# Block two's expert layer: fp32 up-projections for the small experts, one weight matrix per transfer, four fixed experts

## The chip, the cores and the metric

The kernel runs on one core of one Trainium2 chip. The metric is the device time of one execution in microseconds (us). Before the change it is 2680.42 us, the median of three runs (2679.35 to 2682.9). A core has TensorE (PE for its matmuls, PEld for its loads of the stationary operand), VectorE (DVE), ScalarE (ACT), GpSimd (POOL) and SyncE (SP, which here only issues transfers).

## The reference, cut to what matters

Two transformer blocks run one after the other on 1024 tokens of width 1024, all in float32. Each ends in a layer of experts. The change touches the one of block two: 32 experts in 4 groups of 8, two experts for every token, hidden width 256.

```python
def hier_moe_2(x, wg, bg, we, be, w_gate, w_up, w_down):
    g_logits = xf @ wg + bg                      # a group for each token
    grp = jnp.argmax(g_logits, axis=-1)
    e_in = ...                                   # the logits of its 8 experts
    top_v, top_i = lax.top_k(e_in, 2)
    combine = p_grp * jax.nn.softmax(top_v)
    ...
    hb = jax.nn.silu(xb @ w_gate[e]) * (xb @ w_up[e])   # 1024 -> 256, twice
    return hb @ w_down[e]                                # 256 -> 1024
    # each row times its weight, then added to its token
```

The weights of one expert are three matrices of 1 MB each, so 32 experts read 100 MB.

## The kernel before

`run` goes through both blocks in program order; each engine executes its own list in that order. The expert layer (`moe`, line 1799 on) works through the experts in a fixed order `Lay.order`. Every place p in it has a fixed capacity of rows, `caps[p]`. The first `NP` places are the experts 0, 1, 2 themselves ("fixed"), so their weights can be asked for before the routing is known. The other places hold the remaining experts sorted by their number of rows; which expert that is stands in `idx`, and SP must first read it (`values_load`, line 1784) to form the address. Rows beyond a capacity are left to a loop behind (`moe_rest`).

In block two the capacities are 128, 128, 128 (fixed), 192, three of 128, four of 96, six of 80 and fifteen of 64. The order of work is 0, 1, 2, then alternately a larger and a small one (3, 17, 4, 18, ..., 16, 30) and at last 31. A place of 192 is worked as two units of 128 and 64 rows, so there are 18 larger units and 15 small experts (capacity 64, `whole`).

What an expert costs on each engine:

- `gather` (line 1805): POOL fetches the token rows.
- `xT` (line 1815): 8 PE transposes into PSUM; ACT and DVE take them out as a high part and the remainder, both in fp32r, a 4-byte float type whose matmul is one record in the trace. For a small expert both parts lie side by side, so that one stationary operand of 128 columns holds 64 high and 64 low rows.
- `up` (line 1839): four weight stages. A stage has two chunks of `w_gate` in the first 512 columns and two of `w_up` in the others, by two transfers of 256 KB (2 KB per partition each). `w_split` splits it: ACT writes the high part (line 190), DVE the remainder (line 194). A larger unit takes three matmuls for each of 8 chunks (high by high, high by low, low by high), each 512 columns wide. A small expert takes two for each chunk (both parts at once by high, then by low), 16 of 512 columns.
- `hT` (line 1872): the hidden rows of the expert before are transposed, in the middle of `up`.
- `down` (line 1893): two stages of `w_down` of 512 KB. A larger unit takes 12 matmuls of 512 columns. A small expert uses the unsplit weights in fp32: 4 matmuls of 64 by 512, which TensorE carries out as 8 records. ACT scales both halves of the result (line 1916); POOL adds the rows to the output in memory (`put`, line 1796).

Weight stages are taken from a queue (`w`, line 205). Before each take, `w_ahead` asks for the transfers of up to 20 further stages and has 3 further stages split. All large tiles come from one pool of 42; a tile is handed out again when its last reader is done. During the first experts a generator (`gen`) also puts the rest of the routing between the steps.

Of the kernel before, what the change touches and what calls it, by code (L numbers as in the profile page):

```python
# [14 lines left out]
OP = mybir.AluOpType  # L15
# [61 lines left out]
class Lay:  # L77
# [13 lines left out]

    def whole(self, p):
        return self.add and self.caps[p] <= self.small


    def two(self, p, n):
        return n <= self.small and (not self.add or self.whole(p))

    def units(self, p):
        c, b = self.caps[p], self.base[p]  # L100
# [24 lines left out]
class Kern:  # L125
# [1644 lines left out]
    def plan_moe(self, w1, w3, w2, lay, box):  # L1770
        a1 = w1.rearrange("e (p kk k) h -> e kk p (k h)", kk=4, k=2)
        a3 = w3.rearrange("e (p kk k) h -> e kk p (k h)", kk=4, k=2)
        a2 = w2.rearrange("e (k p) d -> e k p d", k=2)
        lo, hi, al = (lambda t: t[:, 0:512]), (lambda t: t[:, 512:1024]), (lambda t: t[:, 0:1024])
        val = {}

        def src(a, p, k):
            if p < lay.NP:
                return a[p, k]

            def go(dst):
                if p not in val:
                    val.clear()
                    val[p] = self.nc.values_load(
                        box["r"]["idx"][0:1, 2, p:p + 1], engines=[mybir.EngineType.SP], min_val=0, max_val=lay.E - 1)
                self.sy.dma_start(dst, a[bass.ds(val[p], 1), k].rearrange("o p f -> (o p) f"))
            return go
        for p in lay.order:
            for kk in range(4):
                self.w_add([(lo, src(a1, p, kk)), (hi, src(a3, p, kk))], 1024)  # L1790
            for k2 in range(2):
                self.w_add([(al, src(a2, p, k2))], 1024, None if lay.whole(p) else lay.small > 0 and not lay.add and k2 == 1)


    def put(self, ys, ix, y):
# [3 lines left out]
    def moe(self, r, vs, late=None):  # L1799
        ac, ve, te, gp = self.ac, self.ve, self.te, self.gp  # L1800
        lay = r["lay"]
        ys = self.ys[lay.E]
        X, Hn, HT, XG, WK = {}, {}, {}, {}, {}
# [11 lines left out]
        def xT(b):  # L1815
            X[b] = []
            for x, idn, s, n in XG.pop(b):
                if lay.two(b, n):
                    xx = self.t(F32R)[:, :16 * n].rearrange("p (k j n) -> p k j n", k=8, j=2)
                    ps = self.p()  # L1820
                    for k in range(8):
                        te.transpose(ps[:, k * n:(k + 1) * n], x[:, k * 128:(k + 1) * 128], idn)
                    pv = ps[:, :8 * n].rearrange("p (k n) -> p k n", k=8)
                    ac.activation(xx[:, :, 0, :], pv, AF.Copy)
                    ve.tensor_sub(xx[:, :, 1, :], pv, xx[:, :, 0, :])
                    X[b].append((xx, None, s, n))
                    continue
                xh, xl = self.t(F32R), self.t(F32R)
                m = 512 // n
                for q in range(0, 8, m):  # L1830
                    ps, w = self.p(), min(m, 8 - q) * n
                    for k in range(q, min(q + m, 8)):
                        te.transpose(ps[:, (k - q) * n:(k - q + 1) * n], x[:, k * 128:(k + 1) * 128], idn)
                    sl = slice(q * n, q * n + w)
                    ac.activation(xh[:, sl], ps[:, :w], AF.Copy)
                    ve.tensor_sub(xl[:, sl], ps[:, :w], xh[:, sl])
                X[b].append((xh, xl, s, n))

        def up(b, mid=None):
            U = X.pop(b)  # L1840
            P = [self.p() for _ in U]
            for kk in range(4):
                if kk == 2 and mid is not None:
                    hT(mid)
                wh, wl = self.w()
                next(gen, None)
                for k in range(2):
                    for ps, (xh, xl, s, n) in zip(P, U):
                        c = 2 * kk + k
                        if xl is None:  # L1850
                            ops = [(xh[:, c].rearrange("p j n -> p (j n)"), w) for w in (wh, wl)]
                        else:
                            ops = [(x[:, c * n:(c + 1) * n], w) for x, w in ((xh, wh), (xh, wl), (xl, wh))]
                        m = 2 * n if xl is None else n
                        for j, (x, w) in enumerate(ops):
                            rhs = w[:, :1024].rearrange("p (w k h) -> p w k h", w=2, k=2)[:, :, k, :]
                            te.matmul(ps[:m].rearrange("p (w h) -> p w h", w=2), x, rhs,  # L1857
                                      start=c == 0 and j == 0, stop=c == 7 and j == len(ops) - 1)
            Hn[b] = []
            for ps, (_, xl, s, n) in zip(P, U):  # L1860
                h = self.h()
                if xl is None:
                    ac.activation(h[:n], ps[n:2 * n], AF.Copy)
                    ve.tensor_add(h[:n], ps[:n], h[:n])
                    ac.activation(h[:n, 0:256], h[:n, 0:256], AF.Silu)
                    ve.tensor_mul(h[:n, 256:512], h[:n, 0:256], h[:n, 256:512])
                else:
                    ac.activation(h[:n, 0:256], ps[:n, 0:256], AF.Silu)
                    ve.tensor_mul(h[:n, 256:512], h[:n, 0:256], ps[:n, 256:512])
                Hn[b].append((h, s, n))  # L1870

        def hT(b):
            HT[b] = []
            for h, s, n in Hn.pop(b):
                ps = self.p()
                for k in range(2):
                    te.transpose(ps[:, k * n:(k + 1) * n], h[:n, 256 + k * 128:256 + (k + 1) * 128], self.idn[:n, :n])
                if lay.whole(b):
                    t = self.h()[:, :2 * n]
                    ac.activation(t, ps[:, 0:2 * n], AF.Copy)  # L1880
                    HT[b].append((t.rearrange("p (k n) -> p k n", k=2), s, n))
                    continue
                t = self.h(F32R)
                tv = t.rearrange("p (k j n) -> p k j n", k=2, j=2)[:, :, :, :n]
                if lay.two(b, n):
                    tv = t[:, :4 * n].rearrange("p (k j n) -> p k j n", k=2, j=2)
                pv = ps[:, 0:2 * n].rearrange("p (k n) -> p k n", k=2)
                ac.activation(tv[:, :, 0, :], pv, AF.Copy)
                ve.tensor_sub(tv[:, :, 1, :], pv, tv[:, :, 0, :])
                t = tv  # L1890
                HT[b].append((t, s, n))

        def down(b):
            W = WK.pop(b)
            for t, s, n in HT.pop(b):
                p0, p1 = self.p(), self.p()
                for k in range(2):
                    wh, wl = W[k]
                    if lay.whole(b):
                        m, ops = n, [(t[:, k, :], wh)]  # L1900
                    elif lay.two(b, n):
                        m, ops = 2 * n, [(t[:, k].rearrange("p j n -> p (j n)"), w) for w in (wh, wl)]
                    else:
                        hh, hl = t[:, k, 0, :], t[:, k, 1, :]
                        m, ops = n, ((hh, wh), (hh, wl), (hl, wh))
                    for j, (a, w) in enumerate(ops):
                        f, e = k == 0 and j == 0, k == 1 and j == len(ops) - 1
                        self.mm(p0[:m], a, w[:, 0:512], f, e)
                        self.mm(p1[:m], a, w[:, 512:1024], f, e)
                y = self.t()  # L1910
                for ps, o in ((p0, 0), (p1, 512)):
                    if lay.two(b, n) and not lay.add:
                        ac.activation(y[:n, o:o + 512], ps[n:2 * n], AF.Copy)
                        ve.tensor_add(y[:n, o:o + 512], ps[:n], y[:n, o:o + 512])
                    elif lay.add:
                        ac.activation(y[:n, o:o + 512], ps[:n], AF.Copy, scale=r["wc"][:n, s[1], b:b + 1])  # L1916
                    else:
                        ac.activation(y[:n, o:o + 512], ps[:n], AF.Copy)
# [6 lines left out]
        gen = r.pop("gen")  # L1925
# [880 lines left out]
    def run(self):  # L2806
        A = self.A
        l1, l2 = self.lays = (
            Lay(2, [192] * 9 + [128] * 7, [0, 1, 9, 2, 10, 3, 4, 11, 5, 12, 6, 13, 7, 14, 8, 15], 64, False),
            Lay(3, [128] * 3 + [192] + [128] * 3 + [96] * 4 + [80] * 6 + [64] * 15,   # L2810
                [0, 1, 2] + [p + q for p in range(3, 17) for q in (0, 14)] + [31], 64, True))
        b1, b2 = {}, {}
        self.plan_one()
        self.plan_moe(A["exp_w1"][0], A["exp_w3"][0], A["exp_w2"][0], l1, b1)
# [61 lines left out]
```

## Time and profile before

| | before |
|---|---|
| median of 3 runs | 2680.42 us (2679.35 to 2682.9) |
| the profiled execution's own time | 2676.59 us |
| its span, first to last instruction | 2674.5 us |
| PE busy | 2484.8 us (93%) |
| DVE, ACT, POOL busy | 1596.0, 1224.4, 608.1 us |
| granted TensorE clock, mean | 0.970 of full speed |
| bytes moved | 378.38 MB, 141 GB/s over the span |

Block two's experts are the last stage: the first transposes of their rows start at 2305.7 us of the span and the last matmul ends at 2658.0 us. A timeline row gives the start, the length to the end of the last of its instructions, and the idle time ahead of it with what ended it. Matmuls overlap, so the cost of one of a row is the distance from this row's start to the next row's start, divided by the count.

### The profile page before, as it was taken

How to read it: one execution, taken by the hardware profiler on the slowest of the kernel's cores; microseconds unless marked ns; L12 is line 12 of the kernel's file. 1: busy time of each engine (PE TensorE's matmuls, PEld its weight loads, DVE VectorE, ACT ScalarE, POOL GpSimd, SP SyncE). 2: the span in 40 equal slices, each digit the busy share in tenths (PEclk: the TensorE clock that was granted, in tenths of full speed). 3: DMA queues.
4: the chain of work that ended last, by engine and by line, in shares of the span. 5: the costliest groups of instructions: out<-in, count | busy, mean ns of one | idle time of the engine just before them, and what ended most of it. 6: DMA issues, size and time to landing. Idle time of an engine off the chain costs nothing. (4 is left out here: it accounts for less than half of the span.)

```text
span 2674.5 us, 35232 instructions
## 1 busy us (share of the span) xinstructions
PE 2484.8 (93%) x12192; PEld 1912.6 (72%) x12192; DVE 1596.0 (60%) x2659; ACT 1224.4 (46%) x2153; POOL 608.1 (23%) x661
## 2 busy tenths in 40 slices
PE   7999999999999799959999999998999989689996
PEld 7976696778877577758788888996655567555543
DVE  4235338842245688765754563567776645777775
ACT  4336521131123477755344243435555532457775
POOL 1011111000001234441000002153655622223221
PEclk9999999999999899979999999998999989899998
DMA  4000243223251689852221221333222265789996
GB/s 136 25 9 10 56 144 104 83 83 103 95 181 72 197 291 311 299 195 86 63 87 48 71 79 26 94 123 113 96 96 77 76 211 178 244 249 341 344 347 218
DMA packets 245877, 378.38 MB, mean 141 GB/s; under 512 B 31344, under 2 KB 142224, under 8 KB 245696
## 3 DMA queue, kind: packets, MB, share of 16 engines
q1 hardware_dynamic: 216720, 282.42, 32.6%
q0 software_dynamic: 28976, 93.67, 11.0%
q8 instruction: 98, 1.61, 0.2%
q14 instruction: 83, 0.68, 0.1%
HBM read 296.65 MB, written 81.99 MB: 142 GB/s over the span
## 5 line engine op out<-in xcount | busy, mean ns | idle before, releaser
L216 PE MATMUL ps<-s,s 128*128 128x512 f32 (+15 forms) x8744 | 1922.4, 379 | 37.1 <-ACT s L212 7.2
L216 PEld LDWEIGHTS ps<-s,s 128*128 128x128 f32 (+6 forms) x8744 | 1502.6, 187 | 416.5 <-issue 95.1
L194 DVE TENSOR_TENSOR s<-s,s 128x1024 fp32r<-128x1024 f32 (+4 forms) x375 | 461.7, 1252 | 437.5 <-ACT s L190 402.0
L190 ACT ACTIVATE s<-s 128x1024 fp32r<-128x1024 f32 (+3 forms) x393 | 391.2, 1034 | 73.7 <-DMA s<-in_w_up 16.4
L1857 PE MATMUL ps<-s,s 128*128 128x512 f32 (+3 forms) x1200 | 319.0, 413 | 28.5 <-DVE s L194 23.3
L1857 PEld LDWEIGHTS ps<-s,s 128*128 128x128 f32 (+3 forms) x1200 | 213.8, 186 | 101.4 <-DVE s L194 36.7
L370 DVE TENSOR_REDUCE mx<-ps 128x1 f32<-128x512 f32 (+10 forms) x304 | 142.4, 505 | 17.1 <-PE ps L216 15.3
L504 ACT ACTIVATE s<-ps 128x512 f32<-128x512 f32 (+1 forms) x192 | 93.8, 489 | 114.4 <-PE ps L216 110.6
L1153 ACT ACTIVATE s<-ps 128x512 f32<-128x512 f32 x24 | 14.3, 598 | 252.0 <-PE ps L216 252.0
L519 POOL TENSOR_TENSOR s<-s,s 128x512 f32<-128x512 f32 (+1 forms) x64 | 108.3, 1692 | 48.5 <-ACT s L506 25.4
L1796 POOL DMA_INDIRECT out<-s,dst x33 | 54.0, 1635 | 244.6 <-ACT s L1916 144.5
L466 PE MATMUL ps<-s,s 128*64 128x512 f32 (+3 forms) x384 | 84.4, 521 | 0.8 <-DVE mx L370 0.8
L1046 DVE SCALAR_TENSOR_TENSOR s<-s,c,s 128x1024 f32<-128x1024 f32 x60 | 82.7, 1379 | 1.5
L1809 POOL DMA_INDIRECT s<-vs,idx x58 | 73.3, 1263 | 43.9 <-issue 10.4
L212 ACT ACTIVATE s<-s 128x512 fp32r<-128x512 f32 (+2 forms) x49 | 36.8, 775 | 76.7 <-DVE s L2329 35.6
L434 ACT ACTIVATE s<-ps 128x512 f32<-128x512 f32 (+4 forms) x112 | 49.3, 447 | 47.7 <-PE ps L216 46.6
L213 DVE TENSOR_TENSOR s<-s,s 128x512 fp32r<-128x512 f32 (+2 forms) x49 | 41.8, 890 | 45.5 <-ACT s L212 45.5
L303 ACT ACTIVATE s<-s 128x1024 f32<-128x1024 f32 (+1 forms) x25 | 26.4, 1055 | 89.1 <-DVE s L1316 46.4
L2305 ACT ACTIVATE s<-ps 128x512 f32<-128x512 f32 x16 | 9.6, 598 | 100.9 <-PE ps L216 100.9
L2352 POOL DMA_DIRECT2D g1s<-s x8 | 4.3, 539 | 226.1 <-ACT s L2306 216.9
L192 POOL TENSOR_TENSOR s<-s,s 128x1024 fp32r<-128x1024 f32 x18 | 47.1, 2618 | 32.0 <-ACT s L190 31.9
L1181 POOL DMA_DIRECT2D ms<-s x8 | 4.3, 533 | 215.9 <-DVE s L1148 161.4
(501 smaller groups left out, 2417.2 us busy)
## 6 DMA issues: line engine op xcount, KB each, us to landing
s<-in_w_in SPq DMA_DIRECT2D x80, 512.0 KB
s<-in_exp_w SPq DMA_DIRECT2D x128, 256.0 KB
s<-in_w_gate SPq DMA_DIRECT2D x128, 256.0 KB
s<-in_w_up SPq DMA_DIRECT2D x128, 256.0 KB
s<-in_w_down SPq DMA_DIRECT2D x64, 512.0 KB
s<-in_exp_w SPq DMA_DIRECT2D x32, 512.0 KB
s<-in_x SPq DMA_DIRECT2D x16, 512.0 KB
ms<-s POOLq DMA_DIRECT2D x16, 512.0 KB, 5.0
```

The costliest lines, as they stand in the source:

```text
L190: self.ac.activation(hi[:, :n], st[:, :n], AF.Copy)
L194: self.ve.tensor_sub(lo[:, :n], st[:, :n], hi[:, :n])
L216: self.te.matmul(out, lhsT, rhs, start=start, stop=stop)
L370: self.ve.tensor_reduce(mx[:, ii, j:j + 1], ps[:, c0 - s0:c1 - s0], axis=AX.X, op=OP.max)
L434: self.ac.activation(pf[:rows, c:], s[:rows, c:], AF.Exp)
L466: self.te.matmul(o[64 * hh:64 * hh + 64, c:], H["v"](j)[:rows], pf[:rows, hh, c:], start=first, stop=last and not c, skip_group_check=True)
L504: self.ac.activation(pf[:rows, hh, c:], s[:rows, c:], AF.Exp)
L519: eng.tensor_tensor(acc[:rows, :, c:], acc[:rows, :, c:], pf[:rows, :, c:], op=OP.add)
L1046: ve.scalar_tensor_tensor(a[:, :T], gl[:, k:k + T], cw[:, c, k:k + 1], a[:, :T], op0=OP.mult, op1=OP.add)
L1796: self.gp.indirect_dma_start(out=ys, out_offset=bass.IndirectOffsetOnAxis(ap=ix, axis=0), in_=y, in_offset=None, bounds_check=T - 1, oob_i ...
L1809: gp.indirect_dma_start(out=x[:n, :D], out_offset=None, in_=vs, in_offset=bass.IndirectOffsetOnAxis(ap=r["idx"][:n, j, b:b + 1], axis=0))
L1857: te.matmul(ps[:m].rearrange("p (w h) -> p w h", w=2), x, rhs, start=c == 0 and j == 0, stop=c == 7 and j == len(ops) - 1)
```

## The change

In block two only:

1. Small experts compute `up` in fp32 too: their rows are copied once, unsplit (DVE), and their weights of all six stages stay unsplit. A new function `up_add` uses 16 matmuls of 256 columns.
2. A stage is now one matrix: one transfer of 512 KB with four rows (4 KB) per partition, in the order gate, up, gate, up, down, down. `up_add` takes a gate and an up stage together and writes the gate to columns 0 to 255 and the up to 256 to 511 of one PSUM bank. A larger unit so takes 48 matmuls of 256 columns where it took 24 of 512. `hT` stands ahead of the second pair of stages, as before in the middle.
3. The second half of a small expert's result is scaled by DVE, no longer by ACT; the steps that added high and low sums of its `up` fall away.
4. Four experts are fixed, with 128 rows each; the place of 192 is now place 4. The sequence of places is the same, so the 192 comes sixth, behind the first small expert, where it was fourth.

```diff
+            if lay.add:
+                for a, n in ((b1, 0), (b3, 0), (b1, 1), (b3, 1), (a2, 0), (a2, 1)):
+                    self.w_add([(al, src(a, p, n))], 1024, None if lay.whole(p) else False)
+                continue
...
-                if lay.two(b, n):
+                if lay.whole(b):
+                    xx = self.t()[:, :8 * n]
+                    ps = self.p()
+                    for k in range(8):
+                        te.transpose(ps[:, k * n:(k + 1) * n], x[:, k * 128:(k + 1) * 128], idn)
+                    ve.tensor_copy(xx, ps[:, :8 * n])
+                    X[b].append((xx, xx, s, n))
+                    continue
+                if n <= lay.small and not lay.add:
...
+        def up_add(b, U, P, mid):
+            for kk in range(2):
+                if kk and mid is not None:
+                    hT(mid)
+                W = [self.w(), self.w()]
+                for k in range(4):
+                    if k % 2 == 0:
+                        next(gen, None)
+                    c = 4 * kk + k
+                    for ps, (xh, xl, s, n) in zip(P, U):
+                        ops = ((xh, 0),) if lay.whole(b) else ((xh, 0), (xh, 1), (xl, 0))
+                        for j, (x, o) in enumerate(ops):
+                            for h, w in enumerate(W):
+                                self.mm(ps[:n, h * 256:h * 256 + 256], x[:, c * n:(c + 1) * n],
+                                        w[o][:, k * 256:(k + 1) * 256], c + j + h == 0,
+                                        c == 7 and h == 1 and j == len(ops) - 1)
...
+                    elif o and lay.whole(b):
+                        ve.tensor_scalar(y[:n, o:o + 512], ps[:n], r["wc"][:n, s[1], b:b + 1], None, op0=OP.mult)
                     elif lay.add:
                         ac.activation(y[:n, o:o + 512], ps[:n], AF.Copy, scale=r["wc"][:n, s[1], b:b + 1])
...
-            Lay(3, [128] * 3 + [192] + [128] * 3 + [96] * 4 + [80] * 6 + [64] * 15, 
+            Lay(4, [128] * 4 + [192] + [128] * 2 + [96] * 4 + [80] * 6 + [64] * 15,
```

On PE, a small expert's `up` between the transposes of the next larger one (`128x80`) and that one's hidden rows stands thus before; `s_22147` and `s_22148` are the high and low part of a stage, `s_22089` the rows:

```order
L1833 MATMUL ps<-c_74,s_21762 128x80 x8
L1857 MATMUL ps<-s_22147,s_22089 128x512
L1857 MATMUL ps<-s_22148,s_22089 128x512
...
L1857 MATMUL ps<-s_22173,s_22089 128x512
L1857 MATMUL ps<-s_22174,s_22089 128x512
...
L1877 MATMUL ps<-c_74,s_22157 128x80 x2
L1857 MATMUL ps<-s_22180,s_22089 128x512
L1857 MATMUL ps<-s_22181,s_22089 128x512
```

and thus now, with `s_22078` a gate stage and `s_22094` an up stage, both unsplit:

```order
L1842 MATMUL ps<-c_74,s_22022 128x80 x8
L212 MATMUL ps<-s_22078,s_22336 64x256
L212 MATMUL ps<-s_22094,s_22336 64x256
...
L1905 MATMUL ps<-c_74,s_22421 128x80 x2
L212 MATMUL ps<-s_22134,s_22336 64x256
L212 MATMUL ps<-s_22140,s_22336 64x256
```

Each half keeps 8 matmuls; each writes 64 rows by 256 columns where it wrote 128 by 512, and there is no low part.

A larger unit's `up` on PE, its first chunks before (`s_22247` and `s_22248` high and low weights, `s_22198` and `s_22199` high and low rows):

```order
L1857 MATMUL ps<-s_22247,s_22198 80x512
L1857 MATMUL ps<-s_22248,s_22198 80x512
L1857 MATMUL ps<-s_22247,s_22199 80x512
...
L1857 MATMUL ps<-s_22273,s_22198 80x512
L1857 MATMUL ps<-s_22274,s_22198 80x512
```

and its first chunk now (`s_22277` and `s_22278` the gate's parts, `s_22304` and `s_22305` the up's):

```order
L212 MATMUL ps<-s_22277,s_22238 80x256
L212 MATMUL ps<-s_22304,s_22238 80x256
L212 MATMUL ps<-s_22278,s_22238 80x256
L212 MATMUL ps<-s_22305,s_22238 80x256
L212 MATMUL ps<-s_22277,s_22239 80x256
L212 MATMUL ps<-s_22304,s_22239 80x256
```

Every matmul of 512 columns has become two of 256.

On SP, the place where the fixed experts' transfers end, before (`s_19369` is the last `up` stage of expert 2, `s_19559` the first of place 3):

```order
L180 DMA s_19369<-in_w_gate 128x512
L180 DMA s_19369<-in_w_up 128x512
L180 DMA s_19378<-in_w_down 128x1024
L180 DMA s_19380<-in_w_down 128x1024
L1784 TENSOR_LOAD idx
L1784 ISA x2
L1786 ISA
L1786 DMA s_19559<-in_w_gate 128x512
```

and now:

```order
L176 DMA s_19366<-in_w_down 128x1024
L176 DMA s_19368<-in_w_down 128x1024
L176 DMA s_19376<-in_w_gate 128x1024
L176 DMA s_19378<-in_w_up 128x1024
L176 DMA s_19386<-in_w_gate 128x1024
L176 DMA s_19388<-in_w_up 128x1024
L176 DMA s_19476<-in_w_down 128x1024
L176 DMA s_19478<-in_w_down 128x1024
L1781 TENSOR_LOAD idx
L1781 ISA x2
```

Six transfers, those of expert 3, have moved ahead of the first read of `idx`.

## Rows read from the trace of the kernel before

**Rows 1.** Windows of the expert stage: start and end, length, busy us, clock, DMA.
```profile
core 0: us, PE busy (x) PEld busy (x) DVE busy (x) ACT busy (x) POOL busy (x), PEclk, DMA share, GB/s
2305.70:2400.00 94.30, 80.15 (x353) 57.66 (x354) 68.12 (x119) 57.45 (x82) 23.36 (x16) 0.92 0.85 262
2400.00:2658.10 258.10, 239.02 (x1031) 139.71 (x1029) 191.95 (x232) 192.16 (x279) 65.69 (x46) 1.00 0.99 331
2305.70:2658.10 352.40, 319.17 (x1382) 197.37 (x1382) 260.06 (x350) 249.61 (x360) 89.06 (x62) 0.98 0.95 312
```

**Rows 2.** Waits of PE, 2305 to 2660: total us, times, longest.
```profile
PE ps L1857 <- DVE s L194: 22.5, 29, 1.4
PE ps L216 <- DVE s L1889: 3.7, 1, 3.7
PE ps L216 <- ACT s L1880: 0.7, 1, 0.7
```

**Rows 3.** Timeline of PE, one larger (96) and one small expert: start, length, instructions.
```profile
2496.55 0.88 PE L1833 MATMUL ps<-c,s 96*128 96x96 f32 x8
2497.22 2.09 PE L1857 MATMUL ps<-s,s 128*128 128x512 f32 x8
2499.15 0.33 PE L1877 MATMUL ps<-c,s 96*128 96x96 f32 x2
2499.26 1.40 PE L1857 MATMUL ps<-s,s 128*128 128x512 f32 x5
2501.42 0.97 PE L1857 MATMUL ps<-s,s 128*128 128x512 f32 x3 [0.76 <-DVE s L194]
2502.22 2.92 PE L216 MATMUL ps<-s,s 128*96 128x512 f32 x12
2505.08 0.71 PE L1822 MATMUL ps<-c,s 64*128 64x64 f32 x8
2505.72 3.02 PE L1857 MATMUL ps<-s,s 128*96 128x512 f32 x12
2508.67 0.34 PE L1877 MATMUL ps<-c,s 64*128 64x64 f32 x2
2508.94 3.04 PE L1857 MATMUL ps<-s,s 128*96 128x512 f32 x12
2511.91 3.65 PE L216 MATMUL ps<-s,s 128*64 128x512 f32 x8
2515.49 0.77 PE L1833 MATMUL ps<-c,s 80*128 80x80 f32 x8
```

**Rows 4.** Timeline of PE in the router, fp32 of 128 columns.
```profile
2240.29 3.69 PE L1258 MATMUL ps<-s,rw 128*36 128x128 f32 x32
2243.91 3.05 PE L216 MATMUL ps<-s,s 128*128 128x512 f32 x12
```

**Rows 5.** Timeline of PE in an earlier projection, fp32r of 256 columns.
```profile
1202.79 12.06 PE L216 MATMUL ps<-s,s 128*128 128x256 f32 x96
```

**Rows 6.** Groups by form, 2150 to 2674: busy us, mean ns, idle before.
```profile
L194 DVE TENSOR_TENSOR s<-s,s 128x1024 fp32r<-128x1024 f32 x168 | 202.1, 1232 | 71.7 <-ACT s L190 37.8 <-ACT s L1916 14.9 <-DMA out<-s,dst 12.2
L190 ACT ACTIVATE s<-s 128x1024 fp32r<-128x1024 f32 x168 | 172.0, 1055 | 48.1 <-DMA s<-in_w_up 16.4 <-PE ps L1857 11.8 <-DMA s<-in_w_out 11.5
L1857 PEld LDWEIGHTS ps<-s,s 128*128 128x128 f32 x408 | 74.9, 197 | 46.1 <-DVE s L194 26.3 <-ACT s L190 3.3 <-DVE s L1836 1.6
```

**Rows 7.** Waits of PE, 2305 to 2400 alone.
```profile
PE ps L1857 <- DVE s L194: 4.5, 5, 1.4
```

**Rows 8.** Timeline of PE: pauses in the first experts.
```profile
2305.72 1.97 PE L1833 MATMUL ps<-c,s 128*128 128x128 f32 x8 [7.40 <-DMA s<-vs,idx]
2377.82 1.43 PE L1857 MATMUL ps<-s,s 128*128 128x512 f32 x5 [0.61 <-DVE s L194]
2397.26 1.61 PE L1857 MATMUL ps<-s,s 128*128 128x512 f32 x3 [1.40 <-DVE s L194]
```

**Rows 9.** Waits of SP's queue, 2270 to 2660: total us, times, longest.
```profile
SPq L1784 <- DVE idx L1565: 19.5, 1, 19.5
```

More of the change, by code (lines that the diff above doesn't have):

```diff
@@ L93, in whole @@
         return self.add and self.caps[p] <= self.small
-    def two(self, p, n):
-        return n <= self.small and (not self.add or self.whole(p))
     def units(self, p):
@@ L1773, in plan_moe @@
         a2 = w2.rearrange("e (k p) d -> e k p d", k=2)
+        b1, b3 = (w.rearrange("e (p kk k) h -> e kk p (k h)", kk=2, k=4) for w in (w1, w3))
         lo, hi, al = (lambda t: t[:, 0:512]), (lambda t: t[:, 512:1024]), (lambda t: t[:, 0:1024])
@@ L1791, in plan_moe @@
             for k2 in range(2):
-                self.w_add([(al, src(a2, p, k2))], 1024, None if lay.whole(p) else lay.small > 0 and not lay.add and k2 == 1)
+                self.w_add([(al, src(a2, p, k2))], 1024, k2 == 1)
     def put(self, ys, ix, y):
@@ L1841, in up @@
             P = [self.p() for _ in U]
[L1842 to L1858, printed above, removed]
+            if lay.add:
+                up_add(b, U, P, mid)
+            else:
+                for kk in range(4):
+                    wh, wl = self.w()
+                    next(gen, None)
+                    for k in range(2):
+                        for ps, (xh, xl, s, n) in zip(P, U):
+                            c = 2 * kk + k
+                            if xl is None:
+                                ops = [(xh[:, c].rearrange("p j n -> p (j n)"), w) for w in (wh, wl)]
+                            else:
+                                ops = [(x[:, c * n:(c + 1) * n], w) for x, w in ((xh, wh), (xh, wl), (xl, wh))]
+                            m = 2 * n if xl is None else n
+                            for j, (x, w) in enumerate(ops):
+                                rhs = w[:, :1024].rearrange("p (w k h) -> p w k h", w=2, k=2)[:, :, k, :]
+                                te.matmul(ps[:m].rearrange("p (w h) -> p w h", w=2), x, rhs,
+                                          start=c == 0 and j == 0, stop=c == 7 and j == len(ops) - 1)
             Hn[b] = []
@@ L1884, in hT @@
                 tv = t.rearrange("p (k j n) -> p k j n", k=2, j=2)[:, :, :, :n]
-                if lay.two(b, n):
+                if n <= lay.small and not lay.add:
                     tv = t[:, :4 * n].rearrange("p (k j n) -> p k j n", k=2, j=2)
@@ L1900, in down @@
                         m, ops = n, [(t[:, k, :], wh)]
-                    elif lay.two(b, n):
+                    elif n <= lay.small and not lay.add:
                         m, ops = 2 * n, [(t[:, k].rearrange("p j n -> p (j n)"), w) for w in (wh, wl)]
@@ L1911, in down @@
                 for ps, o in ((p0, 0), (p1, 512)):
-                    if lay.two(b, n) and not lay.add:
+                    if n <= lay.small and not lay.add:
                         ac.activation(y[:n, o:o + 512], ps[n:2 * n], AF.Copy)
                         ve.tensor_add(y[:n, o:o + 512], ps[:n], y[:n, o:o + 512])
+                    elif o and lay.whole(b):
+                        ve.tensor_scalar(y[:n, o:o + 512], ps[:n], r["wc"][:n, s[1], b:b + 1], None, op0=OP.mult)
                     elif lay.add:
@@ L2809, in run @@
             Lay(2, [192] * 9 + [128] * 7, [0, 1, 9, 2, 10, 3, 4, 11, 5, 12, 6, 13, 7, 14, 8, 15], 64, False),
-            Lay(3, [128] * 3 + [192] + [128] * 3 + [96] * 4 + [80] * 6 + [64] * 15,
-                [0, 1, 2] + [p + q for p in range(3, 17) for q in (0, 14)] + [31], 64, True))
+            Lay(4, [128] * 4 + [192] + [128] * 2 + [96] * 4 + [80] * 6 + [64] * 15,
+                [0, 1, 2, 3, 17] + [p + q for p in range(4, 17) for q in (0, 14)] + [31], 64, True))
         b1, b2 = {}, {}
```

## The prediction

> **What bounds the kernel now.** I first cut the stage of block two's experts into windows [rows 1]. From the first transposes at 2305.7 us to the end of the last matmul at 2658.1 us PE is busy 319.2 of 352.4 us. The reader is to see two parts. Up to 2400 PE is idle 94.3 - 80.15 = 14.1 us, with the transfers at 262 GB/s. From 2400 on it is busy 239.0 of 258.1 us, and the transfers, too, are at a share of 0.99 and 331 GB/s; DVE and ACT are at 192 of 258, so they are not full. PE and the weight stream are nearly balanced, and the question is which of them gets more work.
>
> Next the waits of PE [rows 2]: 22.5 of its idle time are 29 short waits for a split weight, none over 1.4 us. DVE has slack, so behind most of these stands a transfer. The others are single waits, 3.7 us in the first experts and 0.7 at the end among them.
>
> Last the timeline of one pair of experts [rows 3]. It gives the price of every piece, start to start: 12 fp32r matmuls of 512 columns of a larger unit's `down` take 2505.08 - 2502.22 = 2.86 us, 12 of its `up` 2.95 or 2.97 us (0.246 to 0.248 each). Half a small expert's `up` (8) takes 1.93 us, 0.241 each. A small expert's `down`, 4 fp32 matmuls of 512 columns in 8 records, takes 2515.49 - 2511.91 = 3.58 us, 0.895 each. So fp32 costs 3.7 times as much for the same number of columns. The pair takes 18.9 us, and 0.76 of that is a wait.
>
> **The change, part by part.**
>
> *Small experts' `up` in fp32.* Sixteen fp32r matmuls of 512 columns go: 16 x 0.241 = 3.86 us. Sixteen fp32 matmuls of 256 columns with 64 stationary columns come. The trace has none of that width. Its neighbours are 0.895 for 512 columns [rows 3] and (2243.91 - 2240.29) / 16 = 0.226 for 128 (32 records are 16 matmuls) [rows 4]; these are the ends. Per column they agree, 1.75 and 1.77 ns, so I take half of the 512 price, 0.4475. Then 16 x 0.4475 = 7.16 us, 3.30 more per expert, and for 15 experts +49.5 us. It is all on PE, which executes in order and has 33 us idle in the whole stage, so it can't be hidden.
>
> *Larger units' `up` in matmuls of 256 columns.* An earlier projection has 96 such matmuls in a row, each with its own load of 128 columns: 12.06 us, 0.1256 each [rows 5]. Two of them are 0.251 against 0.244 (the mean of the 12 of `down` and of `up` over 12: 2.93 us). 24 x 0.007 = 0.17 us per unit, 18 units: +3.1 us. Ends: 0 (no loss from halving), and +22 us if each of the 48 costs 0.025 more than that row, a fifth.
>
> A load of 128 columns takes 197 ns on the mean in this stage [rows 6], and there are now two for each 512 columns. In rows 5 the loads don't show: 0.1256 a matmul is less than one load's duration, so they run beside the matmuls. The Trainium skill (TensorE: Matmul & The Clock Gate, "Part 3: Packing small matmuls — row/col tiling", under "The mechanism") says that a weight load overlaps matmuls in flight only where the row groups differ; here all use all rows, so by that rule the loads would be paid, and that is the second rival. The trace disagrees with it.
>
> *Splits.* A small expert had four stages split; 15 x 4 = 60 of each kind go: 60 x 1.055 = 63 us of ACT and 60 x 1.232 = 74 us of DVE [rows 6]. Both engines have slack already, so the direct gain is nothing. What it buys is that PE no longer waits for a split in a small expert, and that fewer of the 42 tiles are held.
>
> *PE's waits.* PE gets 52.6 us more work for the same bytes. In the second part the stream moved 331 x 258.1 = 85.4 MB; over 283 us that is 302 GB/s, under what it reached. So PE becomes the only bound there and the stream runs ahead: the 19.1 us idle of this part go but for the 0.7 at the end (the last small expert's `hT`, which nothing covers): -18.4 us. Each pause also cost the emptying of PE: five matmuls ahead of one take 1.40 us where five at 0.244 are 1.22 [rows 3], 0.18; for the 24 pauses of this part (29 less the five for a split's remainder before 2400 [rows 7]) -4.3 us. Of the first part's 14.1 us, five waits for a split, 5.6 us (four for its remainder, one for its high part), from 2377.82 to 2397.26 stand in small experts [rows 8]; those go, I count -5 us, as one of them may remain as a wait for the transfer. The other 8.5 us belong to the first three experts, whose splits and routing steps stay as they are.
>
> *Transfers.* One of 512 KB replaces two of 256 KB, so SP issues 6 instead of 10 for an expert. Cost and gain nothing: PE covers it. With that cover gone the stream would set the end, and the gain would be bounded by the 19 us that PE now waits.
>
> *Four fixed experts.* SP waited 19.5 us for `idx` before the first transfer of place 3 [rows 9]. That wait moves behind six more transfers. PE's first transposes wait for the gathered rows, not for weights (7.40 us [rows 8]); the first three experts' weights are asked for earlier in both. The six transfers are 3.1 MB, 9.5 us at 331 GB/s, inside those 19.5 us as far as tiles are free. I take 0, with ends of -3 us (the gather finds an emptier stream) and +3 us (it finds a fuller one). The 192 rows at place 4 instead of 3 are the same work.
>
> *Small experts' copies.* One DVE copy replaces an ACT and a DVE pass; the second half of the result is scaled by DVE instead of ACT. That scale waits for PE's `down`, and splits for the next larger expert are queued behind it on DVE. These are taken three stages ahead, and PE has the next small or larger `up` to do meanwhile, several us: nothing.
>
> *Sum.* 49.5 + 3.1 - 18.4 - 4.3 - 5.0 = +24.9 us. The profiled execution took 2676.6 us, so 2701.5; the median shown stands 3.8 higher, so the forecast on its scale is 2705 us.
>
> **The rivals.**
>
> 1. *The pauses stay.* The share of 0.99 from 2400 on speaks for it: if the stream still decides, for want of free tiles, PE pays its extra work on top. Against it: nothing PE waits for needs more bytes than before, and PE is slower. Time: +52.6 with no wait gone, 2733 us.
>
> 2. *Loads are paid.* If every matmul of 256 columns costs its load, 48 x 0.197 = 9.46 us instead of 24 x 0.244 = 5.86: 3.6 us a unit, 18 units +65 in place of +3.1, 2767 us. Rows 5 speak against it.
>
> 3. *fp32 at 256 columns is cheap, and the kernel gets faster.* If such a matmul costs 0.241, as one fp32r matmul of 512 columns does, the small experts' `up` adds nothing and the rest of the sum stands: 3.1 - 18.4 - 4.3 - 5.0 = -24.6, 2656 us. It decides below 0.344 a matmul, where 16 of them cost 1.64 us more than before and 15 experts just eat the waits. For it: no row has this width. Against it: both neighbours lie on one line through 0.45.
>
> 4. *The change doesn't keep to the layout.* If the fixed expert 3 had over 128 rows, the loop behind would run a pass that the trace of before doesn't have: at least a gather of 7.4 us, six splits of 2.3 us, 36 matmuls of 0.244 us, some 30 us in a row, 2735 us. The routing worked out from the reference's inputs gives expert 3 115 rows.
>
> **How the numbers follow.** My forecast has 0.80, the rivals 0.10, 0.04, 0.04 and 0.02. The forecast's own spread is from +14 us (every pause of the stage goes with its emptying, but for the last 0.7) to about +40 (half the pauses stay, or halving costs a few us more): 2694 to 2720. Of the 0.10 of the first rival some lies below 2733. The range 2692 to 2724 leaves out rivals 2 to 4 and part of the first. A measurement of this kernel can tell 0.2% from no change, 5.4 us: faster 0.04 (rival 3), same 0.02 (between rival 3 and the floor of +14), slower 0.94.
>
> **What would show it.** In the profile after: a small expert's `up` as 32 fp32 records over 7.2 us, halves of 3.6 us; a larger unit's `up` at 6.0 us with matmuls of 256 columns 0.126 apart; a pair of 96 and 64 at about 21.4 us; PE busy over 97% from 2400 on, its waits for L194 (now the DVE line of `w_split`) under 3 us in total there; the DMA share under 0.95. It is wrong if the fp32 matmul of 256 columns lies far off 0.45 us, if PE still pauses by 15 us or more after 2400, or if the stage's start moves by more than 3 us.

## The result and the profile after

The changed kernel takes 2705.82 us (median of 4 runs, 2698.04 to 2706.94), the kernel before beside it 2679.89 us (2676.19 to 2682.9). The ratio is 1.0091 [1.0068, 1.0114], so it is slower, by 24 us. The forecast was 2705 us. The profiled execution is the one of 2698.04 us, the fastest of its four; its span is 2696.3 us.

Page of the kernel after, busy time of each engine:

```profile
PE 2528.9 (94%) x12864; PEld 1966.3 (73%) x12864; DVE 1531.5 (57%) x2599; ACT 1141.9 (42%) x2048; POOL 601.9 (22%) x661
```

PE gained 44.1 us; DVE and ACT lost 64.5 and 82.5 us. The 60 stages that are no longer split account for 74 and 63 us by the prices of [rows 6]; the rest is steps of the small experts that fell away or moved from ACT to DVE.

Windows of the expert stage after, from the first transposes to the last matmul (columns as in [rows 1]):

```profile
2298.89:2400.00 101.11, 88.64 (x535) 72.74 (x536) 65.16 (x118) 49.68 (x72) 23.32 (x19) 0.93 0.79 259
2400.00:2679.10 279.10, 278.73 (x1521) 181.40 (x1519) 130.56 (x174) 118.79 (x184) 60.73 (x47) 1.00 0.87 291
2298.89:2679.10 380.21, 367.37 (x2054) 254.14 (x2054) 195.71 (x290) 168.47 (x255) 84.05 (x66) 0.98 0.85 283
```

The stage is 27.8 us longer than in [rows 1]: PE is busy 48.2 us more, and idle 12.8 instead of 33.2 us, 20.4 less. After 2400 PE is idle for 0.4 us in all, and the transfers, at a share of 0.99 before, are at 0.87. Nearly all the idle time that is left lies ahead of 2400.

Waits of PE after, 2285 to 2690 (to [rows 2] and [rows 7]):

```profile
PE ps L212 <- DVE s L190: 7.5, 6, 2.6
PE ps L1842 <- DMA s<-vs,idx: 5.6, 1, 5.6
PE ps L1643 <- DVE s L1639: 3.6, 1, 3.6
PE ps L212 <- ACT s L186: 1.3, 2, 0.7
PE ps L212 <- ACT s L1908: 0.4, 1, 0.4
```

L212 is now the line of the matmuls; L190 (DVE) and L186 (ACT) are the two halves of a split. The 24 pauses after 2400 are gone. But ahead of it 8.8 us of waits for weight splits (7.5 and 1.3) stand where 6.4 stood (4.5 and 1.9), one of 2.6 us.

Timeline of PE after, one larger (96) and one small expert (to [rows 3]):

```profile
2480.07 0.88 PE L1842 MATMUL ps<-c,s 96*128 96x96 f32 x8
2480.88 3.67 PE L212 MATMUL ps<-s,s 128*64 128x256 f32 x16
2484.48 0.39 PE L1905 MATMUL ps<-c,s 96*128 96x96 f32 x2
2484.80 6.60 PE L212 MATMUL ps<-s,s 128*64 128x256 f32 x28
2491.32 0.71 PE L1823 MATMUL ps<-c,s 64*128 64x64 f32 x8
2491.97 3.07 PE L212 MATMUL ps<-s,s 128*96 128x256 f32 x24
2494.97 0.34 PE L1905 MATMUL ps<-c,s 64*128 64x64 f32 x2
2495.23 6.64 PE L212 MATMUL ps<-s,s 128*96 128x256 f32 x32
2501.81 0.88 PE L1842 MATMUL ps<-c,s 96*128 96x96 f32 x8
```

Row 2 is half of a small expert's `up`: 8 matmuls in 16 fp32 records, 2484.48 - 2480.88 = 3.60 us, 0.45 each. Row 6 is half of a larger unit's: 24 matmuls of 256 columns in 3.00 us. (The rows of 28 and 32 run on into `down`.) The pair takes 21.74 us and holds no wait, where it took 18.9.

Timeline of PE after, pauses in the first experts:

```profile
2310.44 0.50 PE L212 MATMUL ps<-s,s 128*128 128x256 f32 x2 [0.69 <-ACT s L186]
2313.54 2.10 PE L212 MATMUL ps<-s,s 128*128 128x256 f32 x9 [2.60 <-DVE s L190]
...
2334.04 4.28 PE L212 MATMUL ps<-s,s 128*128 128x256 f32 x21 [1.82 <-DVE s L190]
...
2373.11 5.53 PE L212 MATMUL ps<-s,s 128*128 128x256 f32 x45 [1.54 <-DVE s L190]
```

All four stand at the beginning of a half of `up`, whose first matmuls use the high parts of the gate and the up stage and then the two remainders. The first row waits, after one matmul, for the high part of the up stage; the other three wait after three matmuls, for the remainder of the up stage, the second of the two taken together. Where the split of one stage of both matrices was enough for the next 6 matmuls of 512 columns, PE now needs the splits of two stages before its fourth matmul of 256.

### The profile page after: what moved, and what is told of

The parts are those of the page before. It is cut to its first block, busy times and chain, and to the rows that moved or that the text cites. A ratio compares the mean times of both kernels' runs of the same rounds, so it can differ in the third digit from the quotient of the medians.

```text
span 2696.3 us, 35820 instructions
## 1 busy us (share of the span) xinstructions
PE 2528.9 (94%) x12864; PEld 1966.3 (73%) x12864; DVE 1531.5 (57%) x2599; ACT 1141.9 (42%) x2048; POOL 601.9 (22%) x661
## 3 DMA queue, kind: packets, MB, share of 16 engines
q0 software_dynamic: 28976, 93.67, 10.9%
## 5 line engine op out<-in xcount | busy, mean ns | idle before, releaser
L212 PE MATMUL ps<-s,s 128*128 128x512 f32 (+16 forms) x10088 | 2146.1, 372 | 43.2 <-DVE s L190 9.9
L212 PEld LDWEIGHTS ps<-s,s 128*128 128x128 f32 (+8 forms) x10088 | 1671.6, 183 | 461.7 <-issue 98.6
L190 DVE TENSOR_TENSOR s<-s,s 128x1024 fp32r<-128x1024 f32 (+3 forms) x315 | 390.8, 1258 | 425.5 <-ACT s L186 416.6
L186 ACT ACTIVATE s<-s 128x1024 fp32r<-128x1024 f32 (+4 forms) x333 | 329.6, 1030 | 59.6 <-PE ps L212 19.7
L1885 PE MATMUL ps<-s,s 128*128 128x512 f32 x528 | 131.7, 406 | 2.1 <-ACT s L186 0.8
L1149 ACT ACTIVATE s<-ps 128x512 f32<-128x512 f32 x24 | 14.3, 598 | 252.0 <-PE ps L212 252.0
L1885 PEld LDWEIGHTS ps<-s,s 128*128 128x128 f32 x528 | 100.0, 193 | 26.5 <-DVE s L190 1.4
L1896 ACT ACTIVATE s<-ps 128x256 f32<-128x256 f32 (+3 forms) x49 | 18.6, 380 | 91.6 <-PE ps L212 60.4
L188 POOL TENSOR_TENSOR s<-s,s 128x1024 fp32r<-128x1024 f32 x18 | 48.1, 2674 | 32.0 <-ACT s L186 31.9
L1946 ACT ACTIVATE s<-ps,s 64x512 f32<-64x512 f32 (+3 forms) x51 | 32.9, 681 | 50.4 <-PE ps L212 35.1
```

The source lines that it names most:

```text
L186: self.ac.activation(hi[:, :n], st[:, :n], AF.Copy)
L190: self.ve.tensor_sub(lo[:, :n], st[:, :n], hi[:, :n])
L212: self.te.matmul(out, lhsT, rhs, start=start, stop=stop)
```

## The experiments

Ratios are to the kernel before, run beside each on the same chip; a ratio of 0.0010 is 2.7 us.

**One part alone, or left out.** The first kernel has the four fixed experts and nothing else of the change.

```diff
-            Lay(3, [128] * 3 + [192] + [128] * 3 + ...
+            Lay(4, [128] * 4 + [192] + [128] * 2 + ...
```

> The kernel before with the four fixed experts and their capacities alone. My theory (TensorE covers the transfers, and the first transposes wait for gathered rows): no change, within 3 us of before, about 2680 us. Rival (the six transfers moved ahead of the read of idx help the first experts): 5 to 8 us faster, about 2673 us, with the pauses between 2377 and 2397 us gone.

Measured: 2680.13 us, ratio 0.999 [0.9975, 1.0005]. The fourth fixed expert costs nothing that can be told from zero.

The second keeps everything of the change but the fp32 `up`: the small experts' rows and gate and up stages are split again, 32 matmuls of 256 columns.

```diff
-    self.w_add([(al, src(a, p, n))], 1024, None if lay.whole(p) else False)
+    self.w_add([(al, src(a, p, n))], 1024, None if lay.whole(p) and a is a2 else False)
...
-    ops = ((xh, 0),) if lay.whole(b) else ((xh, 0), (xh, 1), (xl, 0))
+    ops = ((xh, 0), (xh, 1)) if lay.whole(b) else ((xh, 0), (xh, 1), (xl, 0))
```

> The changed kernel with the small experts' up in fp32r on split weights again (32 matmuls of 256 columns); one matrix per stage and four fixed experts stay. My theory (the fp32 matmuls are the whole loss): TensorE gets 15 x (7.2 - 32 x 0.125) = 48 us less work, some pauses come back, so between 2658 us (none) and 2684 us (all), most likely 2675. Rival (the halved matmuls with twice the weight loads, or the one-matrix stages, are the loss): it stays above 2695 us.

Measured: 2706.79 us, 1.0096 [1.0065, 1.0127]. My theory fell here: without its largest cost the kernel is no faster. Its window after 2400 and its waits of PE, 2285 to 2700:

```profile
2400.00:2685.90 285.90, 252.29 (x1533) 187.95 (x1531) 200.50 (x243) 185.58 (x266) 69.65 (x49) 0.95 0.88 293
```

```profile
PE ps L212 <- DVE s L190: 37.4, 34, 4.5
PE ps L212 <- ACT s L186: 7.9, 4, 3.7
```

PE is idle 33.6 us there, though the transfers are at 0.88 and not at their limit: it waits for splits that are late for another reason.

The third is the kernel before with only the small experts' `up` in fp32, on its old stages of both matrices (an `up` of 8 fp32 matmuls of 512 columns).

```diff
+    elif lay.whole(b):
+        ops = [(xh[:, c*n:(c+1)*n], wh)]
...
-    self.w_add([(lo, src(a1, p, kk)), (hi, src(a3, p, kk))], 1024)
+    self.w_add([(lo, src(a1, p, kk)), (hi, src(a3, p, kk))], 1024, None if lay.whole(p) else False)
```

> The kernel before with only the small experts' up in fp32 on unsplit weights: 8 fp32 matmuls of 512 columns in place of 16 of fp32r, old stages, three fixed experts. My theory: 8 x 0.895 = 7.16 us instead of 3.86, 49.5 us in 15 experts, less the pauses of some 28 us: about 2702 us, with a small expert's up as 16 records. Rival (the loss comes from the stages of one matrix): about 2680 us or less.

Measured: 2697.1 us, 1.006 [1.004, 1.0081], some 16 us of the 24. Its window after 2400:

```profile
2400.00:2674.80 274.80, 274.12 (x1013) 127.22 (x1012) 120.61 (x160) 125.52 (x195) 56.80 (x46) 1.00 0.93 307
```

PE is full as in the kernel after. So fp32 alone already makes PE the bound, and the rest of the loss, some 8 us with intervals that overlap, should have another source.

The fourth is the changed kernel without half of the small experts' `up`.

```diff
+    if lay.whole(b) and k in (1, 2):
+        continue
```

> The changed kernel that leaves out half of the small experts' up (8 of the 16 fp32 matmuls of each; its values are then incomplete), all transfers kept. My theory (TensorE alone sets the end): 15 x 3.6 = 54 us less work, so faster than after by 25 us or more, down to where the weight stream sets the end, between 2652 and 2680 us. Rival (the weight stream already sets the end of the changed kernel): under 10 us faster than after, 2695 us or more.

Measured: 2672.15 us, 0.9961 [0.9946, 0.9976]. Some 54 us of matmuls are gone (15 x 3.6), and the kernel is 35 us faster than the changed one by the ratios. Its window after 2400:

```profile
2400.00:2649.50 249.50, 240.16 (x1313) 155.89 (x1311) 129.65 (x174) 118.12 (x184) 61.26 (x47) 0.99 0.97 329
```

The transfers are back at 0.97 and 329 GB/s, and PE pauses again by 9.3 us: behind PE stands the stream, as in the kernel before.

**Two stages at once, or one.** Each half of `up` takes a gate and an up stage together. Two kernels take them one after the other, the gate's four chunks, then the up's: the changed kernel, and the one with split small experts.

```diff
-                W = [self.w(), self.w()]
-                for k in range(4):
...
-                            for h, w in enumerate(W):
+                for h in range(2):
+                    w = self.w()
+                    next(gen, None)
+                    for k in range(4):
```

> The changed kernel, but up takes one stage at a time: all matmuls of the gate's four chunks, then those of the up's. My theory (taking a gate and an up stage together holds two more pairs of split tiles and makes TensorE wait for two splits at once; with fp32 small experts this costs some 8 us in the first four experts and nothing later): about 8 us faster than after, 2697 us, with the waits for a split's remainder ahead of 2400 us down from 7.5 to about 2 us. Rival (the rest of the loss over the fp32 matmuls is the halving itself): no change, 2705 us.

> The changed kernel with small experts in fp32r on split weights, and up taking one stage at a time. My theory (the pair of stages is what made the split version wait): TensorE's work is that of before plus some 4 us for the halved matmuls, the waits fall from 45 us to those of before, about 25: 2680 to 2688 us. Rival (splits are late for any stage of one matrix, whose transfer must land whole): it stays at 2700 us or more.

Measured: the changed kernel takes 2694.71 us so, 1.0055 [1.0041, 1.0069], as little as with fp32 alone; the other 2717.82, 1.0147 [1.0132, 1.0161], even slower than in pairs. The windows of the first:

```profile
2301.47:2400.00 98.53, 91.03 (x566) 74.02 (x566) 66.21 (x119) 52.72 (x76) 28.49 (x20) 0.95 0.85 273
2400.00:2674.13 274.13, 273.76 (x1491) 177.71 (x1489) 128.39 (x171) 115.26 (x180) 58.87 (x46) 1.00 0.88 294
```

Its idle time ahead of 2400 is 7.5 us instead of 12.5, and its stage takes 372.7 instead of 380.2 us. PE's waits for weight splits ahead of 2400 fall from 8.8 to 3.7 us, so the new waits of the first experts come from the pairs. For the kernels with split small experts my guess that the pairs were the cause was wrong. What their queue waits for says more. Waits of SP's queue, 2400 to 2640, in the kernel before, then in the second kernel (split, pairs), then with one stage at a time:

```profile
SPq L1786 <- DMA s<-in_w_down: 33.2, 35, 3.6
SPq L1786 <- DMA s<-in_w_up: 21.5, 19, 2.8
SPq L1786 <- DMA s<-in_w_gate: 16.8, 32, 2.8
```

```profile
SPq L1783 <- PE ps L212: 54.2, 33, 5.1
SPq L1783 <- DMA out<-s,dst: 42.3, 9, 6.3
SPq L1783 <- DVE s L190: 28.7, 16, 6.4
```

```profile
SPq L1783 <- PE ps L212: 91.2, 50, 5.4
SPq L1783 <- DVE s L190: 42.3, 23, 5.2
```

Before, SP waits for earlier transfers to land: the stream is at its limit. In the other two it waits for the last reader of a tile, a matmul, a split, or the adding of a result's rows to the output: no tile is free. DVE's waits in the second kernel, 2400 to 2690, say it of the splits themselves:

```profile
DVE s L190 <- DMA out<-s,dst: 26.5, 9, 7.1
```

A split writes two tiles of the same 42. None is free while 20 stages are asked for ahead, and the split waits until a result is written and its tile comes back. With one stage at a time the trace doesn't show this: DVE waits 3.4 us for results there, and ACT's half of the split sits idle for 43.6 us in 11 waits (2400 to 2660) whose end the profile does not name.

The kernel before asks for 20 ahead and splits as many stages as these two; why does its pool not run dry? How far ahead SP really is can be counted in the traces: the stages that it has asked for, from the expert whose `up` comes next, at the transposes ahead of that `up`. In the kernel before they are 18 just after 2400 and 6 to 8 from 2534 on; with four fixed experts alone they fall in the same way, from 20 to 6 to 9. In the two kernels with split small experts they are 18 to 22 all the way. So the kernel before does not hold the tiles of 20 stages there. Its queue's main waits are the 86 for landings above, 71.5 us. Every one of them ends with the transfer eight places earlier, and a stage of both matrices takes two of those eight places. With fp32 on these old stages (the third experiment) the count is 14 or 15 for all but the last experts, and 18 to 25 in the changed kernel. This fits that one transfer to a stage lets the queue run so far ahead that the pool is empty; no run changes the transfers alone, so it is not shown.

**How far ahead.** If that is so, fewer stages ahead must make these kernels faster. The split kernel with pairs, and the kernel before, with 14 in place of 20:

```diff
-MLS, MLP, MLD, MLX = 3, 3, {16: 8, 32: 20}, {16: 2, 32: 5}
+MLS, MLP, MLD, MLX = 3, 3, {16: 8, 32: 14}, {16: 2, 32: 5}
```

> The changed kernel with small experts in fp32r on split weights, stages taken in pairs, but transfers asked for 14 stages ahead in place of 20. My theory (the 42 tiles run out: splits wait for a tile that a scattered result still holds, 26.5 us on VectorE): six tiles more are free, those waits shrink below 8 us, 10 to 20 us faster than with 20 ahead, about 2690 us. Rival (two splits at once are simply late, or the stream is): no change or slower, 2706 us or more.

> The kernel before with transfers asked for 14 stages ahead in place of 20. My theory (there the stream decides after 2400 us, TensorE's waits end with a landing transfer, and VectorE hardly waits for a tile): a shallower queue can only let the stream run dry in the first experts, so no change to 5 us slower, 2680 to 2685 us. Rival (its waits, too, come from tiles that run out): 5 to 15 us faster.

Measured: the split kernel takes 2674.49 us, 0.9978 [0.9968, 0.9987], 32 us less than with 20 ahead, which is more than I had expected. Its window after 2400, SP's waits, 2400 to 2640, and what is left of DVE's waits for results, 2400 to 2690:

```profile
2400.00:2656.56 256.56, 237.10 (x1466) 172.79 (x1464) 194.37 (x235) 175.72 (x255) 66.51 (x46) 0.99 0.95 323
```

```profile
SPq L1783 <- DMA s<-in_w_up: 37.5, 30, 3.5
SPq L1783 <- DMA s<-in_w_gate: 33.6, 32, 2.8
SPq L1783 <- PE ps L212: 32.8, 28, 3.3
```

```profile
DVE s L190 <- DMA out<-s,dst: 0.5, 1, 0.5
```

The stream is the bound again, SP waits for transfers first, and the splits' 26.5 us of waits for results are 0.5. The results themselves land about as fast as before (median 7.6 us instead of 8.5, 2400 to 2660), so quicker writes are not what ended these waits. The kernel before hardly moves: 2672.47 us, 0.9986 [0.9972, 1.0]; at the depth that it really reached, its pool did not starve it.

Then the split kernel with one stage at a time and 14 ahead, the changed kernel itself with 14 ahead, and the split kernel with pairs and 10 ahead (10 in place of 14 in this line):

```diff
-MLS, MLP, MLD, MLX = 3, 3, {16: 8, 32: 20}, {16: 2, 32: 5}
+MLS, MLP, MLD, MLX = 3, 3, {16: 8, 32: 14}, {16: 2, 32: 5}
```

> Small experts in fp32r on split weights, stages taken one at a time, 14 stages ahead in place of 20. My theory (tiles that run out made the version with 20 ahead slow; the order of the matmuls is harmless): it falls from 2718 us to the level of the version with pairs and 14 ahead, 2670 to 2676 us, and TensorE's waits for splits fall from 49 us below 25. Rival (one stage at a time is itself bad for split small experts): 2690 us or more.

> The changed kernel with 14 stages ahead in place of 20, nothing else. My theory (TensorE alone sets its end after 2400 us, and only the pauses of the first four experts, 9 us, can shrink): 2696 to 2704 us, at most 9 us faster than after. Rival (tiles that run out cost the changed kernel as much as the version with split small experts): 2680 us or less.

> Small experts in fp32r on split weights, stages taken in pairs, 10 stages ahead; with 20 it took 2706.8 us, with 14 2674.5. My theory (from 14 down the tiles suffice and the stream is the next bound, so a shallower queue only loses cover): 2674 to 2682 us. Rival (tiles still run out at 14): under 2670 us.

Measured: 2668.14 us, 0.9952 [0.9939, 0.9965], for the first, which beats both kernels; 2690.08, 1.0033 [1.0021, 1.0045], for the second; 2678.16, 0.9991 [0.9981, 1.0001], for the third, so 10 gains nothing over 14. The first's window of the stage:

```profile
2304.49:2649.55 345.06, 320.71 (x2054) 248.35 (x2054) 270.96 (x365) 240.15 (x345) 92.16 (x66) 0.97 0.93 312
```

That is 7.3 us shorter than [rows 1] at the same 312 GB/s and about the same PE time: only pauses went. The changed kernel gained 15 us by the ratios, more than I had allowed. Of this its trace shows 8.4 in the stage (371.8 us), 5.6 of it idle time ahead of 2400 and 2.9 less busy time; the rest is not settled, as the profiled execution of the changed kernel lies 7.8 us under that kernel's median.

Last, the changed kernel with one stage at a time and 14 ahead:

> The changed kernel (small experts in fp32) with stages taken one at a time and 14 stages ahead; beside the run with split small experts, one at a time, 14 ahead (2668.1 us) it differs by the fp32 alone. My theory: 15 x (7.2 - 4.0) = 48 us more work, against 17.3 us of waits and the emptying of TensorE at 25 of them (4.5 us) that go: +26 us, about 2694 us, TensorE busy over 99% after 2400 us. Rival (with enough tiles the fp32 version gains as much as the split one did from one stage at a time, or the fp32 matmuls hide more than the waits): 2680 us or less.

```diff
-                W = [self.w(), self.w()]
+                for h in range(2):
+                    w = self.w()
...
-MLS, MLP, MLD, MLX = 3, 3, {16: 8, 32: 20}, {16: 2, 32: 5}
+MLS, MLP, MLD, MLX = 3, 3, {16: 8, 32: 14}, {16: 2, 32: 5}
```

Measured: 2690.74 us, 1.0044 [1.0031, 1.0058]. Its window of the stage:

```profile
2300.93:2671.30 370.37, 365.41 (x2054) 252.96 (x2054) 195.44 (x290) 168.04 (x255) 80.17 (x66) 0.98 0.88 290
```

It is as fast as with pairs at that depth. PE is busy 365.4 of 370.4 us, so hardly anything but PE's own work is left in the stage. The kernel stands 25 us above the split one with the same stages (1.0044 against 0.9952).

The kernels with one matrix to a stage and four fixed experts, in one table (median us, ratio):

| small experts' `up` | stages taken | 20 ahead | 14 ahead |
|---|---|---|---|
| fp32, unsplit | in pairs | 2705.82, 1.0091 (the change) | 2690.08, 1.0033 |
| fp32, unsplit | one at a time | 2694.71, 1.0055 | 2690.74, 1.0044 |
| fp32r, split | in pairs | 2706.79, 1.0096 | 2674.49, 0.9978 |
| fp32r, split | one at a time | 2717.82, 1.0147 | 2668.14, 0.9952 |

## Why the prediction was right, and where not

- **Small `up` in fp32, +49.5 us: right.** 3.60 us a half, 7.2 an expert, where 3.86 stood: 3.34 x 15 = +50.1 us. The price of such a matmul, taken as 0.4475, is 0.45. Rival 3 (0.241 for such a matmul) fell with it.
- **Halved matmuls, +3.1 us: small, as said.** 24 take 3.00 us where 12 of 512 columns took 2.95 or 2.97 [rows 3], under 0.1 us a unit, 1 to 2 us in all. Rival 2, that the doubled weight loads are paid, would have shown 3.9 us in that row: a load of 96 columns takes 0.162 us on the mean after the change, and 24 of them stand there. The sentence of the Trainium skill behind it (TensorE: Matmul & The Clock Gate, "Part 3: Packing small matmuls — row/col tiling", "The mechanism") says that a load overlaps matmuls in flight only where the row groups differ. It does not hold in this trace: all of these matmuls use all rows.
- **Pauses after 2400 go, -18.4 and -4.3 us: right.** 19.1 us idle became 0.4, with the transfers at 0.87. Rival 1 (they stay) fell. Added work less the emptying was 52.6 - 4.3 = 48.3 us; PE's busy time in the stage grew by 48.2. The experiment without half of the small `up` shows the far side: there the pauses and the full stream return.
- **First part, -5.0 us: the step that failed.** "Five waits for a split, 5.6 us [...], from 2377.82 to 2397.26 stand in small experts [rows 8]; those go", and "the other 8.5 us belong to the first three experts, whose splits and routing steps stay as they are." The first is a misreading. Rows of the kernel before around these waits:

```profile
2376.08 0.71 PE L1822 MATMUL ps<-c,s 64*128 64x64 f32 x8
...
2381.13 0.49 PE L1857 MATMUL ps<-s,s 128*128 128x512 f32 x1 [1.88 <-ACT s L190]
2382.39 1.45 PE L1857 MATMUL ps<-s,s 128*128 128x512 f32 x5 [0.76 <-DVE s L194]
2383.76 0.47 PE L1877 MATMUL ps<-c,s 64*128 64x64 f32 x2
```

The `up` between the transposes of a small expert (L1822) and the hidden rows of the small expert before it (L1877, 64x64) is a larger unit's, and it runs 12 matmuls in this half. So three of the five waits, 3.2 us, stand in a larger unit, and only 2.4 us in a small expert. The 2.4 went; in the larger unit 1.5 us stayed. The second did not hold either: the idle time of the experts ahead of it grew from 8.5 to 10.9 us. Its waits for weight splits went from 0.8 to 7.2 us, since `up` now needs two stages split, while a wait of 3.7 us for hidden rows fell to 0.2. In all 14.1 us became 12.5, not 9.1, and the stage grew by 27.8 and not by 24.9 us. Taking one stage at a time takes 5.0 us of this idle time away, 7.5 us of the stage and 10 us of the time (1.0091 to 1.0055).
- **Four fixed experts, 0: right**, 0.999 [0.9975, 1.0005] alone. I had also said that a stage start more than 3 us off would prove me wrong; it is 6.8 us earlier. Of this 5.0 us had arisen by 2217, in code that is the same in both, and 1.8 in the wait for the gathered rows (5.62 instead of 7.40 us [rows 8]).
- **How near the total came: in part luck.** The profiled execution is 21.5 us slower than the one before (2698.04 and 2676.59): 27.8 in the stage, 2.9 more than forecast, less the 6.8 of the earlier start, which no term had. It lies 7.8 us under its median where the forecast, going by the one before, put 3.8. These misses nearly cancel, and so 2705 meets 2705.82.
- **"Fewer of the 42 tiles are held": said, and not priced.** The prediction counted this as nothing, and the transfers too ("Cost and gain nothing"). With the small experts' stages split as before, the other parts of the change cost 26 us by themselves (2706.79 us, 1.0096), where my terms for them were +3.1 for halving and 0 for the rest; with 14 ahead these 26 us are gone (2674.49). The forecast of the whole did not meet this cost, most likely because fp32 without splits came in the same change and needs fewer tiles. That was luck: the prediction had not asked whether the tiles suffice.

## What to carry to other kernels

Price a matmul of an unseen width by its columns from the two nearest rows, and then see which of the engine and the stream has less left over: that decides whether added work is paid. Where buffers come from one pool, an edit that needs fewer of them can hide what others cost, so the prices of its parts do not add (here 16 us for fp32 alone, 26 for the rest alone, 24 for both). When the queue that issues loads waits for readers and results instead of earlier loads, the stream is below its best rate, and PE waits for splits all the same, asking for less ahead can be faster. The depth that a program asks for is not the depth that its queue reaches: count it in the trace. And before a wait is put to one unit, look at which transposes and hidden rows stand around it.

## What the hardware did that I had not expected

The long pauses cost more than their length. Timeline of PE in the split kernel with pairs and 20 ahead (second experiment), and its windows of 4 us around the first of these pauses:

```profile
2406.13 0.39 PE L212 MATMUL ps<-s,s 128*128 128x256 f32 x1
2410.24 0.50 PE L212 MATMUL ps<-s,s 128*128 128x256 f32 x2 [3.72 <-ACT s L186]
...
2415.25 2.64 PE L212 MATMUL ps<-s,s 128*128 128x256 f32 x12
2417.83 0.34 PE L1899 MATMUL ps<-c,s 64*128 64x64 f32 x2
```

```profile
2404.00:2408.00 4.00, 2.52 (x16) 1.43 (x14) 1.03 (x1) 0.00 (x0) 0.00 (x0) 1.00 1.03 299
2408.00:2412.00 4.00, 1.00 (x4) 0.80 (x5) 2.99 (x5) 3.15 (x5) 0.00 (x0) 0.83 0.36 117
2412.00:2416.00 4.00, 4.00 (x28) 3.91 (x27) 2.25 (x3) 3.46 (x6) 1.57 (x1) 0.50 0.63 154
2416.00:2420.00 4.00, 4.00 (x29) 3.80 (x28) 2.79 (x8) 1.81 (x3) 0.00 (x0) 0.82 0.84 176
```

Ahead of the pause, and in it, the granted clock is full (2.4 GHz); after 3.72 us without a matmul it falls, and stands at 0.50 (1.2 GHz) from 2412 to 2416, when PE already works again. 12 matmuls of 256 columns take 2417.83 - 2415.25 = 2.58 us here, where 24 take 3.0 at full clock. For the whole stage the same 2054 rows of PE take 333.6 us busy in that kernel and 320.7 in the fastest one, so 13 of the 40 us between their stages (385.6 and 345.1) are the same matmuls taking longer; the granted clock of the stage is 0.94 in the one and 0.97 in the other. The kernel before, with 24 pauses of at most 1.4 us after 2400, kept 1.00 there [rows 1].
